# Hybrid attention trunk: query and key tiles in pairs, memory heads first, attention outputs kept in DRAM

## The chip, the cores and the metric

The kernel runs on one core of one Trainium2 chip. The metric is the device time of one execution in microseconds (us); lower is better. Engines are named as in the profile: PE is TensorE (PEld its weight loads), DVE VectorE, ACT ScalarE, POOL GpSimd, SP the SyncE queue from which the loads are issued.

## What is computed

Two layers over 512 tokens of width 2048, all in float32. Cut to what matters here:

```python
for l in range(DEPTH):                                   # 2
    h = rms_norm(x, norm_g[l])
    z = h @ w_in[l]                                      # q, k, v, gate of 6 NA, 6 DL heads; q, gate of 4 memory heads
    o_na = neighbourhood_attention(na_q, na_k, na_v, na_rpb[l])
    o_dl = dilated_attention(rope(dl_q, pos), rope(dl_k, pos), dl_v)
    mk, mv = split(mem_n @ w_mem_kv[l])                  # 256 memory tokens
    o_m = memory_attention(m_q, mk, mv)
    y = concat([o_na * silu(na_g), o_dl * silu(dl_g), o_m * silu(m_g)])
    x = x + y @ w_out[l]
return rms_norm(x, final_g)
```

A head is 128 wide, so it is one column tile of a weight matrix. The contraction over 2048 is cut in 16 k-tiles of 128.

## The kernel before

**Products.** Each float32 operand is split in a high and a low part (`split`, lines 219 to 223: a cast on ACT, a subtraction on DVE). `mm3` (line 243) makes a product with three matmuls: high by high, high by low, low by high. A plain column tile (`gemm_t`) is 16 k-tiles by three matmuls of 512 columns, 48 in all. The values (`gemm_v`) have the tokens as stationary operand and four tiles at once.

**Weights.** They come in halves of 128x1024 in the fixed order `SEQ`; `next_half` loads and splits three halves ahead of the product that uses them. All loads are issued by SP, in program order.

**Pairs.** `gemm_two` makes two column tiles together. Of k-tiles 0 to 7 it takes `PAIRS` = 4 pairs (k, k+4) as two-by-two block matrices: columns of the two tiles, the two halves of the tokens. Seven products of half width (256 columns) stand in the place of eight. Three of the seven use sums of weights (made by `combine` on DVE), three use sums of activations (`mix_pair`), and the parts are added on the way out: `part` is the PSUM bank of the shared products, `e1` and `e2` the corrections, `first` and `second` the main sums. Before, only the gate tiles 4 to 13 and most of the output tiles go in pairs.

**Order.** In a layer: values of heads 0 to 3 (`v0`), NA heads 0 to 3 (q and k each a plain tile), memory values (`mv`), memory keys and queries with their four heads, `v1`, NA 4 and 5, DL 0 and 1, `v2`, DL 2 to 5, 16 gate tiles, 16 output tiles. Attention is not a stage: `attend` (line 405) queues the score products, the transposes and the value products of a head as `steps` that `pump` puts between the matmuls of the next tiles when a running count of PE time (`clock`) reaches them. The times are in `NA_TIMES`, `DIL_TIMES`, `MEM_TIMES`: time to the first score, distance of steps, wait for the transposes. DVE takes the scores out of PSUM with the bias (line 460), ACT does the exponential (line 450), DVE the division (452, 453), PE transposes (418), ACT and DVE split the result (`pth`, `ptl`), PE multiplies by the values into `pv`. A tile scheduler then fixes the order on every engine; each engine works strictly down its own list.

**Norms.** In `v0` the squares are summed in `ssq`; `rms_sums` multiplies them by ones on PE (line 385), a chain of 12 small DVE operations makes the reciprocal root (`rsqrt`, 370 to 376), DVE scales the identity by it (391), and `rms_rows` spreads it over the rows on PE (399). For memory tokens `memory_tile` (line 540) loads two tiles, splits them on ACT and DVE (line 228) and in layer 0 sums squares in `macc` on POOL (365). Before, memory tiles are split beside NA head 3 and `mv`.

**Outputs of attention** stay in SBUF tiles of pool `u` (63 buffers) until the gates multiply them.

Of the kernel before, what the change touches and what calls it, by code (L numbers as in the profile page):

```python
# [33 lines left out]
U_BUFS = 63  # L34
PAIRS = 4
PLAIN = 2
GATES = range(4, 14)
ASIDE = (2, 3)
# [4 lines left out]
NA_TIMES = (5.0, 1.2, 3.0)  # L43
DIL_TIMES = (8.0, 1.3, 4.0)
# [35 lines left out]
def hybrid_kernel(ctx: ExitStack, tc: tile.TileContext, xT, memT, gains, rpbw, wts, cs_tab, dil_tab, na_tab, outT):  # L80
# [65 lines left out]
    for _ in range(WARM):  # L146
        nc.tensor.matmul(bank[:, :P], lhsT=ones, rhs=ones, start=True, stop=True)
    xs = dpool.tile([KO, P, T], F32, tag="xs", name="xs")


    stream = []
    for layer in range(NL):
        at = 0
        two_by_two = {"o": range(PLAIN, KO if layer + 1 < NL else KO - LAST), "g": GATES}
        for key in SEQ:
            tiles = 4 if key[0] in ("v", "mv") else 1
            if key[1] not in two_by_two.get(key[0], ()):
                stream += [(layer, key, (at + i // 2, i % 2)) for i in range(2 * tiles)]
            elif key[1] % 2 == 0:

                two = {}
                stream += [(layer, key, (at, 1)), (layer, key, ("raw", two, at)), (layer, key, (at + 1, 1))]
                stream += [(layer, key, (part, two)) for part in ("sums", "sum", "differences")]
            at += tiles
# [34 lines left out]
    def combine(layer, part, two, at=None):  # L199

        hi, lo = f32rt("wh", W_BUFS, W_HALF), f32rt("wl", W_BUFS, W_HALF)
        if part == "raw":
            a, b, s1 = f32t("wr", W_BUFS, W_HALF), f32t("wr", W_BUFS, W_HALF), tmp()
            two.update(a=a, b=b, s1=s1)
            nc.sync.dma_start(out=a, in_=wts[layer, at, :, :W_HALF])
            nc.sync.dma_start(out=b, in_=wts[layer, at + 1, :, :W_HALF])
            split(a, hi, lo)
            nc.vector.tensor_tensor(s1, b[:, :T], b[:, T:], ALU.add)  # L210
            nc.vector.tensor_tensor(b[:, :T], b[:, :T], a[:, :T], ALU.add)
            nc.vector.tensor_tensor(a[:, :T], a[:, :T], s1, ALU.add)
            nc.vector.tensor_tensor(a[:, T:], a[:, T:], a[:, :T], ALU.add)
            return hi, lo
        if part == "sum":
            return split(two["s1"], hi[:, :T], lo[:, :T])
        return split(two["a" if part == "sums" else "b"], hi, lo)
# [33 lines left out]
    def gemm_t(l, key, act, n=T):  # L251

        acc = acc_bank()
        for half in range(2):
            hi, lo = next_half(l, key)
            for k8 in range(8):
                ko = half * 8 + k8
# [5 lines left out]
    def gemm_two(l, key, act, mixed):  # L263
# [6 lines left out]
        def plain(acc):  # L270
            hi, lo = next_half(l, key)
            for k8 in range(8):
                sl = slice(k8 * P, (k8 + 1) * P)
                mm3(acc, (hi[:, sl], lo[:, sl]), act[8 + k8], k8 == 0, False)
                pump()

        def product(out, w, c0, b, start=False, stop=False, shared=False):
            for i in range(PAIRS):
                sl = slice(c0 + i * P, c0 + (i + 1) * P)
                mm3(out, (w[0][:, sl], w[1][:, sl]), b(i), start and i == 0, stop and i == PAIRS - 1, shared=shared)  # L280
# [8 lines left out]

        e1, e2, u2 = f32t("pth", 2), f32t("pth", 2), tmp(n)  # L290
        plain(first)
        w = next_half(l, key)
        product(part[:, left], w, 0, half_of(0, left), start=True, stop=True, shared=True)
        nc.scalar.copy(e1[:, left], part[:, left])
        product(first[:, left], w, T, half_of(PAIRS, left))
        plain(second)
# [3 lines left out]
        product(first[:, right], w, T, half_of(PAIRS, right), stop=True)  # L300
        product(part[:, right], next_half(l, key), 0, mixed_of(0), stop=True, shared=True)
        nc.vector.tensor_tensor(e1[:, right], part[:, right], u2, ALU.add)
        w = next_half(l, key)
# [3 lines left out]
        product(second[:, left], w, T, mixed_of(2), stop=True)  # L307
        return (first, e1, ALU.add), (second, e2, ALU.subtract)
# [7 lines left out]
    def mix_pair(y, z):  # L316
# [3 lines left out]
        c, d = f32t("p", 4), f32t("p", 4)  # L320
# [84 lines left out]
    def attend(q, score, v, order, first, gap, wait):  # L405
# [16 lines left out]
        def values(n):  # L422
# [22 lines left out]
        return out  # L445
# [18 lines left out]
    def na_head(l, h, q, k, v):  # L464
# [20 lines left out]
        return attend(q, score, v, order, *NA_TIMES)  # L485

    def dil_head(q, k, v):
# [4 lines left out]

        return attend(q, score, v, [(kt, [(qt, kt * P) for qt in range(4)]) for kt in range(4)], *DIL_TIMES)

    def mem_head(q, mk, v):
# [10 lines left out]
        return attend(q, score, v, [(kt, [(qt, kt * P) for qt in range(4)]) for kt in range(2)], *MEM_TIMES)  # L506
# [22 lines left out]
    for l in range(NL):  # L529
# [15 lines left out]
        def beside_first(q):  # L545
# [4 lines left out]
            else:  # L550
# [13 lines left out]
        def beside_mv(q):  # L564
            for _ in range(2 if q in (2, 3) else 0):
                memory_tile()

        def qk_tile(key, scale):
            acc = gemm_t(l, key, act)
            t = tmp()  # L570
            nc.vector.scalar_tensor_tensor(t, acc, scale, rstd, ALU.mult, ALU.mult)
            return split(t, u32r(), u32r())

        def rope_tile(key, scale):
            acc = gemm_t(l, key, act)
            t, u = tmp(), tmp()
            nc.vector.scalar_tensor_tensor(t, acc, scale, rope_c, ALU.mult, ALU.mult)
            nc.vector.scalar_tensor_tensor(u[64:], acc[:64], scale, rope_s[:64], ALU.mult, ALU.mult)
            nc.vector.scalar_tensor_tensor(u[:64], acc[64:], scale, rope_s[64:], ALU.mult, ALU.mult)
            nc.vector.tensor_tensor(t, t, u, ALU.add)  # L580
            return split(t, u32r(), u32r())
# [10 lines left out]
        def memory_heads():  # L592
# [16 lines left out]
            for h in range(H_M):  # L609
                o["m", h] = mem_head(qk_tile(("mq", h), SCALE), mk[h], head_v(mv, h))  # L610

        o = {}
        for n in range(H_NA + H_DL):
            if n == 4:
                memory_heads()
            if n % 4 == 0:
                v = v_split(gemm_v(l, ("v", n // 4), act, 4, beside_first if n == 0 else None,
                                   n == 0 and l == 0), rstd_tok)
                if n == 0:
                    if l == 0:  # L620
                        nc.sync.dma_start(out=namask, in_=na_tab)
                        nc.sync.dma_start(out=dil_sb, in_=dil_tab)
                    nc.sync.dma_start(out=rope_c, in_=cs_tab[0])
                    nc.sync.dma_start(out=rope_s, in_=cs_tab[1])
                    nc.gpsimd.tensor_tensor(rope_c, rope_c, rstd, ALU.mult)
                    nc.gpsimd.tensor_tensor(rope_s, rope_s, rstd, ALU.mult)
            for _ in range(4 if n == 3 else 0):
                memory_tile()
            if n < H_NA:
                q = qk_tile(("naq", n), SCALE)  # L630
                k = qk_tile(("nak", n), 1.0)
                o["na", n] = na_head(l, n, q, k, head_v(v, n % 4))
# [7 lines left out]
        mixed = []  # L640

        def gate(z):

            e = tmp()
            nc.scalar.activation(e, z, AF.Silu)
            y, = o[MIX[len(gated)]]
            out = f32t("ptl", 2) if len(gated) in ASIDE else y
            nc.vector.tensor_tensor(out, y, e, ALU.mult)
            gated.append(out)

        for j in range(KO):
            if j in GATES:
                if j % 2 == 0:
                    for acc, e, op in gemm_two(l, ("g", j), act, mixed):
                        z = f32t("p", 4)
                        nc.vector.tensor_tensor(z, acc, e, op)
                        nc.vector.tensor_tensor(z, z, rstd, ALU.mult)
                        gate(z)
                continue
            acc = gemm_t(l, ("g", j), act)  # L660
            z = tmp()
            nc.vector.tensor_tensor(z, acc, rstd, ALU.mult)
# [204 lines left out]
```

## Time and profile before

| | |
|---|---|
| median of 3 runs | 1847.19 us (1847.12 to 1847.57) |
| the profiled execution's own time | 1847.28 us |
| its span | 1845.5 us |
| PE busy | 1831.0 us, 99% |
| DVE busy | 1086.0 us, 59% |
| ACT busy | 751.1 us, 41% |
| POOL busy | 53.3 us, 3% |
| DMA, mean | 110 GB/s |

The span is the time from the first to the last instruction that the profile holds; the execution's own time is 1.8 us longer. Matmuls overlap at their ends in the trace, so their rate is read from start to start. A busy share is an average over all stages.

### The profile page before, as it was taken

What the parts mean: (1) busy time and instruction counts of PE and PEld (TensorE: products, weight loads), DVE (VectorE), ACT (ScalarE), POOL (GpSimd) and SP (SyncE); (2) the same over time, 40 slices, a digit from 0 to 9 for tenths busy, and PEclk for the clock granted to TensorE, in tenths of its full rate; (3) what the DMA queues carried; (4) which work ended last, traced back from release to release, by engine and by line L of the source; (5) the groups of instructions that cost most, each with busy time, mean ns of one, the idle gap of its engine ahead of it and who ended that gap; (6) DMA issues with size and microseconds to landing.
All of it is one profiled execution on the core that took longest, in us unless ns stands there. A gap on an engine that the chain in (4) does not pass through costs nothing.

```text
span 1845.5 us, 24250 instructions
## 1 busy us (share of the span) xinstructions
PE 1831.0 (99%) x9586; PEld 1569.0 (85%) x9586; DVE 1086.0 (59%) x1803; ACT 751.1 (41%) x1188; POOL 53.3 (3%) x111
## 2 busy tenths in 40 slices
PE   9999999999999999999999999999999999999997
PEld 8888988888888898899888888888888888988987
DVE  7457553463566866666654564435636658676665
ACT  6346442333334434433443453323333444454442
POOL 0113000100000000000000100000000000000000
PEclk9999999999999999999999999999999999999999
DMA  7335423222222233344643353232222222333433
GB/s 283 102 102 156 137 69 98 89 75 86 86 78 81 79 98 121 123 140 160 183 149 96 112 172 114 70 102 81 69 91 80 78 71 80 104 120 115 132 107 110
DMA packets 69201, 202.99 MB, mean 110 GB/s; under 512 B 7264, under 2 KB 16992, under 8 KB 69088
## 3 DMA queue, kind: packets, MB, share of 16 engines
q1 hardware_dynamic: 68800, 201.16, 34.1%
q8 instruction: 75, 1.23, 0.3%
q10 hardware_dynamic: 288, 0.30, 0.1%
q14 instruction: 38, 0.31, 0.1%
HBM read 193.04 MB, written 8.39 MB: 109 GB/s over the span
## 4 chain that ended last, share of the span: by engine, by line
PE 97%; DVE 1%; DMA 0%; issue 0%; ACT 0%; ACTq 0%; DVEq 0%; SPq 0%
PE acc L247 80%; PE sc L247 10%; PE pv L247 4%; PE sc L418 2%; DVE u L228 0%; DVE wl L222 0%; PE acc L342 0%; DVE wr L761 0%; DMA g_sb<-in_gains 0%; DMA u<-in_memT 0%; PE sc L399 0%; PE sc L746 0%; PE sc L385 0%; DVE p L460 0%; ACT u L227 0%
## 5 line engine op out<-in xcount | busy, mean ns | idle before, releaser
L247 PE MATMUL acc<-u,wh 128*128 128x512 f32 (+1 forms) x3976 | 1113.2, 366 | 0.0
L247 PEld LDWEIGHTS acc<-u,wh 128*128 128x128 f32 x3976 | 706.7, 189 | 107.4
L247 PE MATMUL acc<-u,wl 128*128 128x512 f32 (+1 forms) x1988 | 724.7, 365 | 0.0
L222 DVE TENSOR_TENSOR wl<-wr,wh 128x1024 fp32r<-128x1024 f32 (+1 forms) x344 | 420.8, 1223 | 371.9 <-ACT wh L221 370.6
L221 ACT CAST wh<-wr 128x1024 fp32r<-128x1024 f32 (+1 forms) x344 | 360.6, 1048 | 541.4 <-PE acc L247 436.1
L247 PEld LDWEIGHTS acc<-u,wl 128*128 128x128 f32 x1988 | 375.2, 189 | 61.2
L247 PE MATMUL acc<-wh,u 128*128 128x512 f32 x880 | 283.0, 391 | 0.0
L247 PEld LDWEIGHTS acc<-wh,u 128*128 128x128 f32 x880 | 165.2, 188 | 33.7 <-DVE u L228 0.3
L247 PE MATMUL acc<-wl,u 128*128 128x512 f32 x440 | 171.5, 390 | 0.0
L247 PE MATMUL sc<-u,wh 128*128 128x256 f32 x736 | 138.3, 286 | 0.0
L222 DVE TENSOR_TENSOR ptl<-sc,pth 128x512 fp32r<-128x512 f32 (+2 forms) x112 | 67.5, 603 | 93.6 <-ACT pth L221 93.1
L247 PEld LDWEIGHTS sc<-u,wh 128*128 128x128 f32 x736 | 117.3, 191 | 5.2
L221 ACT CAST pth<-sc 128x512 fp32r<-128x512 f32 (+2 forms) x112 | 57.9, 517 | 123.3 <-PE sc L418 122.7
L247 PE MATMUL sc<-u,wl 128*128 128x256 f32 x368 | 104.1, 283 | 0.0
L247 PEld LDWEIGHTS acc<-wl,u 128*128 128x128 f32 x440 | 82.7, 188 | 16.2
L450 ACT ACTIVATE p<-p,stat 128x256 f32<-128x256 f32 (+1 forms) x96 | 59.2, 616 | 86.9 <-DVE stat L460 86.1
L247 PE MATMUL sc<-u,u 128*128 128x256 f32 (+1 forms) x384 | 80.5, 322 | 0.0
L247 PEld LDWEIGHTS sc<-u,u 128*128 128x128 f32 x384 | 65.3, 188 | 11.6
L247 PEld LDWEIGHTS sc<-u,wl 128*128 128x128 f32 x368 | 70.3, 191 | 0.0
L247 PE MATMUL pv<-pth,u 128*128 128x512 f32 (+2 forms) x224 | 68.4, 386 | 0.0
L221 ACT CAST u<-tmp 128x512 fp32r<-128x512 f32 (+1 forms) x64 | 37.9, 592 | 68.9 <-DVE tmp L580 67.2
L418 PEld LDWEIGHTS sc<-ident,p 128*128 128x128 f32 x376 | 47.8, 140 | 15.2 <-DVE p L453 0.6
(137 smaller groups left out, 1201.0 us busy)
## 6 DMA issues: line engine op xcount, KB each, us to landing
wr<-in_wts SPq DMA_DIRECT2D x319, 512.0 KB, 3.6
p<-in_xT SPq DMA_DIRECT2D x23, 256.0 KB, 4.8
p<-xs SPq DMA_DIRECT2D x22, 256.0 KB, 3.4
u<-in_memT SPq DMA_DIRECT2D x16, 256.0 KB, 4.3
xs<-u SPq DMA_DIRECT2D x16, 256.0 KB, 2.0
outT<-wr SPq DMA_DIRECT2D x6, 512.0 KB, 2.9
e<-in_rpbw SPq DMA_DIRECT2D x12, 192.0 KB, 2.4
pth<-in_xT SPq DMA_DIRECT2D x4, 256.0 KB, 4.9
```

The costliest lines, as they stand in the source:

```text
L221: nc.scalar.copy(hi, x)
L222: nc.vector.tensor_tensor(lo, x, hi.bitcast(F32), ALU.subtract)
L247: nc.tensor.matmul(out, lhsT=a[i], rhs=b[j], start=start and n == 0, stop=stop and n == 2, skip_group_check=shared)
L418: nc.tensor.transpose(tr[:, i * P:(i + 1) * P], probs[qt][:, col:col + P], ident)
L450: nc.scalar.activation(s, src, AF.Exp, bias=neg_max, scale=scale, accum_out=l)
```

## The change

1. The two column tiles q and k of each NA and DL head become one pair of `gemm_two` with `QK_PAIRS` = 3 k-pairs: 12 more pairs in a layer. Of the gates tile 0 and 1 (3 k-pairs) and tiles 2 to 13 (4) are pairs; 14 and 15 stay plain.
2. Memory values, keys and queries come right behind `v0`. Memory tiles are split in the second half of `v0` and the first half of `mv`. The sums of activations are built beside the first two memory queries, the fourth behind gate pair 0.
3. `attend` writes a head's output to a DRAM tensor `ys` from ACT's queue (32 writes of 256 KB), and `head` reads it back on SP before the gate (32 reads). The mask of NA and the tables of rope become `u` tiles that are loaded in each layer; the pool has 66.
4. `combine` adds and splits only the columns of the k-pairs taken; the corrections `e1`, `e2` are completed inside `gemm_two`, which hands the result to `take`. The part-left product of its last half is now the last matmul group of a pair.
5. The first score of a head waits longer: `NA_TIMES` 7.0 for 5.0, `DIL_TIMES` 11.0 for 8.0.

```diff
-U_BUFS = 63
+U_BUFS = 66
+QK_PAIRS = 3
 PAIRS = 4
+TWO = {(s, h): QK_PAIRS for s, n in (("naq", 6), ("dlq", 6)) for h in range(n)}
+TWO |= {("g", j): QK_PAIRS if j == 0 else PAIRS for j in range(0, 14, 2)}
-GATES = range(4, 14)
-NA_TIMES = (5.0, 1.2, 3.0)
-DIL_TIMES = (8.0, 1.3, 4.0)
+NA_TIMES = (7.0, 1.2, 3.0)
+DIL_TIMES = (11.0, 1.3, 4.0)
 SEQ = (
     [("v", 0)]
-    + [(s, h) for h in range(4) for s in ("naq", "nak")]
     + [("mv", 0)]
     + [("mk", h) for h in range(H_M)]
     + [("mq", h) for h in range(H_M)]
+    + [(s, h) for h in range(4) for s in ("naq", "nak")]
...
+        if part == "b":
+            split(b[:, c:], hi[:, c:], lo[:, c:])
+            a1, a2, b1, b2 = a[:, :c], a[:, T:T + c], b[:, :c], b[:, T:T + c]
+            for out, x, y in ((b2, b1, b2), (b1, b1, a1), (a1, a1, b2), (a2, a2, a1)):
+                nc.vector.tensor_tensor(out, x, y, ALU.add)
             return hi, lo
...
+        others = [k for k in range(8) if k % 4 >= ns]
+        plain(first, next_half(l, key), range(8), range(8, KO), True)
...
+        product(part[:, right], w, T, mixed_of(0), stop=True, shared=True)
         nc.vector.tensor_tensor(e1[:, right], part[:, right], u2, ALU.add)
         product(part[:, left], w, 0, mixed_of(3), stop=True, shared=True)
         nc.scalar.copy(e2[:, left], part[:, left])
+        nc.vector.tensor_tensor(e1, first, e1, ALU.add)
+        take(0, e1)
         nc.vector.tensor_tensor(e2[:, right], part[:, right], e2[:, left], ALU.add)
+        nc.vector.tensor_tensor(e2, second, e2, ALU.subtract)
+        take(1, e2)
...
                 nc.scalar.copy(out[0], bank[0])
+                nc.scalar.dma_start(out=ys[MIX.index(name)], in_=out[0])
...
+            if q >= 4:
+                memory_tile()
             at = 6 if l == 0 else 3
             if q == at:
                 diag.append(rms_sums(rstd_tok, T, ssq))
...
+        def turned(x, scale):
+            u = tmp()
+            nc.vector.scalar_tensor_tensor(u[64:], x[:64], scale, rope_s[:64], ALU.mult, ALU.mult)
+            nc.vector.scalar_tensor_tensor(u[:64], x[64:], scale, rope_s[64:], ALU.mult, ALU.mult)
+            nc.vector.scalar_tensor_tensor(x, x, scale, rope_c, ALU.mult, ALU.mult)
+            nc.vector.tensor_tensor(x, x, u, ALU.add)
+            return split(x, u32r(), u32r())
+        def qk_tiles(key, rotate):
+            out = []
+            def take(i, x):
+                scale = (SCALE, 1.0)[i]
+                out.append(turned(x, scale) if rotate else scaled(x, scale, x))
+            gemm_two(l, key, act, mixed, QK_PAIRS, take, u32)
+            return out
...
+        def head():
+            y = u32()
+            nc.sync.dma_start(out=y, in_=ys[len(gated)])
+            gated.append(y)
+            return y
```

**How the order moves, first place.** PE in `v0` of layer 0, from the products of the sums of squares (`sc<-ones,ssq`) to the products that spread the result (`sc<-tmp,ones`); `acc` are the four value tiles. Before, 24 matmuls lie between the two (21 of them are left out here):

```order
L385 MATMUL sc_457<-ones,ssq 128x1 x4
L247 MATMUL acc_106<-wh_293,u_396 128x512
...
L247 MATMUL acc_109<-wl_294,u_400 128x512
L247 MATMUL acc_109<-wh_293,u_401 128x512
L399 MATMUL sc_510<-tmp_475,ones 128x128 x4
L247 MATMUL acc_106<-wh_344,u_443 128x512
```

Now:

```order
L256 MATMUL acc_106<-wl_292,u_406 128x512
L407 MATMUL sc_495<-ones,ssq 128x1 x4
L256 MATMUL acc_106<-wh_291,u_407 128x512
...
L256 MATMUL acc_104<-wh_342,u_468 128x512
L256 MATMUL acc_104<-wh_342,u_471 128x512
L421 MATMUL sc_562<-tmp_513,ones 128x128 x4
L256 MATMUL acc_104<-wl_343,u_471 128x512
```

Of the 24 matmuls 14 are left between the two (11 are left out here): the sums moved back by 14 matmuls, into the middle of their half, and the spreading products by four, into the next half.

**Second place.** DVE in the same stretch now; `rs` and `rstd_tok` are the small chain, `u<-u,g_sb,u` is a memory tile's split, `ssq` the squares, the last row scales the identity:

```order
L387 TENSOR_TENSOR ssq<-ssq,tmp_478 128x512
L392 TENSOR_SCALAR rs_500<-sc_495 128x4
L237 SCALAR_TENSOR_TENSOR u_484<-u_481,g_sb,u_483 128x256
L394 TENSOR_SCALAR rstd_tok<-rs_500 128x4
L396 TENSOR_TENSOR rs_502<-rstd_tok 128x4
L237 SCALAR_TENSOR_TENSOR u_484<-u_481,g_sb,u_483 128x256
L397 SCALAR_TENSOR_TENSOR rs_502<-rs_502,rs_500 128x4
L398 SCALAR_TENSOR_TENSOR rstd_tok<-rs_502,rstd_tok 128x4
L396 TENSOR_TENSOR rs_502<-rstd_tok 128x4
...
L413 TENSOR_SCALAR tmp_513<-ident,rstd_tok 128x128 x4
```

Two memory splits stand inside the chain, where before one weight split stood.

**Third place.** DVE in DL head 3 of layer 0; `ptl` is the low part of a transposed block that PE's value product waits for, `wl` a weight half, `u` and `tmp` the rope of the next tile (lines 577 to 580 before). Before:

```order
L580 TENSOR_TENSOR tmp_4838<-tmp_4838,tmp_4839 128x512
L222 TENSOR_TENSOR wl_4851<-wr_4849,wh_4850 128x1024
L222 TENSOR_TENSOR u_4845<-tmp_4838,u_4844 128x512
L222 TENSOR_TENSOR ptl_4879<-sc_4873,pth_4878 128x512
L222 TENSOR_TENSOR wl_4890<-wr_4888,wh_4889 128x1024
L222 TENSOR_TENSOR ptl_4906<-sc_4900,pth_4905 128x512
L222 TENSOR_TENSOR ptl_4926<-sc_4920,pth_4925 128x512
L222 TENSOR_TENSOR ptl_4947<-sc_4941,pth_4946 128x512
L577 SCALAR_TENSOR_TENSOR tmp_4956<-acc_4848,rope_c 128x512
```

Now (lines 601 to 604 are rope, 231 is the split, 222 a sum of weights):

```order
L604 TENSOR_TENSOR u_4789<-u_4789,tmp_4977 128x512
L601 SCALAR_TENSOR_TENSOR tmp_4988<-u_4790,u_3328 64x512
L602 SCALAR_TENSOR_TENSOR tmp_4988<-u_4790,u_3328 64x512
L231 TENSOR_TENSOR u_4983<-u_4789,u_4982 128x512
L603 SCALAR_TENSOR_TENSOR u_4790<-u_4790,u_3327 128x512
L231 TENSOR_TENSOR wl_5001<-wr_4918,wh_5000 128x640
L604 TENSOR_TENSOR u_4790<-u_4790,tmp_4988 128x512
L222 TENSOR_TENSOR wr_4918<-wr_4918 128x384
L231 TENSOR_TENSOR ptl_5037<-sc_5031,pth_5036 128x512
L231 TENSOR_TENSOR u_4994<-u_4790,u_4993 128x512
L222 TENSOR_TENSOR wr_4918<-wr_4918,wr_4916 128x384
L231 TENSOR_TENSOR ptl_5058<-sc_5052,pth_5057 128x512
```

The last two `ptl` of a head stand behind the rope operations of both tiles of the next head, where before the rope of the second tile came behind all four.

## Rows read from the trace of the kernel before

**Rows 1.** The page, parts 1 and 4: busy time of each engine; the chain that ended last by line.

```profile
PE 1831.0 (99%) x9586; PEld 1569.0 (85%) x9586; DVE 1086.0 (59%) x1803; ACT 751.1 (41%) x1188; POOL 53.3 (3%) x111
...
PE acc L247 80%; PE sc L247 10%; PE pv L247 4%; PE sc L418 2%; DVE u L228 0%; DVE wl L222 0%; PE acc L342 0%; DVE wr L761 0%; DMA g_sb<-in_gains 0%; DMA u<-in_memT 0%; PE sc L399 0%; PE sc L746 0%; PE sc L385 0%; DVE p L460 0%; ACT u L227 0
```

**Rows 2.** Timeline of PE in two gate pairs; start us, busy us, engine, line, operation, tiles, count.

```profile
643.10 0.63 PE L247 MATMUL acc<-u,wh 128*128 128x512 f32 x2
...
644.49 0.62 PE L247 MATMUL acc<-u,wh 128*128 128x512 f32 x2
...
648.57 0.40 PE L247 MATMUL sc<-u,wh 128*128 128x256 f32 x2
...
656.90 0.40 PE L247 MATMUL sc<-u,wh 128*128 128x256 f32 x2
...
659.78 0.40 PE L247 MATMUL sc<-u,wh 128*128 128x256 f32 x2
...
664.22 0.63 PE L247 MATMUL acc<-u,wh 128*128 128x512 f32 x2
```

**Rows 3.** Timeline of PE: the first score product of eight heads (256 wide NA, 512 wide DL).

```profile
131.86 0.52 PE L247 MATMUL sc<-u,u 128*128 128x256 f32 x3
...
158.83 0.52 PE L247 MATMUL sc<-u,u 128*128 128x256 f32 x3
...
334.73 0.52 PE L247 MATMUL sc<-u,u 128*128 128x256 f32 x3
...
361.01 0.52 PE L247 MATMUL sc<-u,u 128*128 128x256 f32 x3
...
390.68 0.84 PE L247 MATMUL sc<-u,u 128*128 128x512 f32 x3
...
419.11 0.84 PE L247 MATMUL sc<-u,u 128*128 128x512 f32 x3
...
549.95 0.84 PE L247 MATMUL sc<-u,u 128*128 128x512 f32 x3
...
579.05 0.84 PE L247 MATMUL sc<-u,u 128*128 128x512 f32 x3
```

**Rows 4.** Timeline of PE: value products of the head beside which memory tiles are split.

```profile
171.01 0.38 PE L247 MATMUL pv<-ptl,u 128*128 128x256 f32 x1 [0.29 <-DVE ptl L222]
...
174.44 0.38 PE L247 MATMUL pv<-ptl,u 128*128 128x256 f32 x1 [0.39 <-DVE ptl L222]
```

**Rows 5.** Timeline by engine: the sums of squares and their rows in the first values stage.

```profile
39.34 0.94 PE L385 MATMUL sc<-ones,ssq 128*128 128x1 f32 x8
...
45.73 1.06 PE L399 MATMUL sc<-tmp,ones 128*128 128x128 f32 x8
...
40.32 0.16 DVE L370 TENSOR_SCALAR rs<-sc 128x4 f32<-128x4 f32 x1 [3.81 <-PE sc L385]
...
45.11 0.87 DVE L391 TENSOR_SCALAR tmp<-ident,rstd_tok 128x128 f32<-128x128 f32 x4
```

**Rows 6.** DVE instructions of line 228: nanoseconds min/median/max, first and last start, form.

```profile
L228 DVE SCALAR_TENSOR_TENSOR u<-u,g_sb,u x32: 469/483/1052, 129.2 to 1083.7; 128x256 fp32r<-128x256 f32 x32
```

**Rows 7.** Busy time of each engine in a stretch of four DL heads: PE, PEld, DVE, ACT, POOL.

```profile
482.00:600.00 118.00, 118.00 (x552) 97.27 (x551) 73.81 (x134) 47.77 (x78) 0.00 (x0) 1.00 0.25 80
```

**Rows 8.** Timeline of DVE in a DL head: rope operations one behind the other.

```profile
559.41 0.69 DVE L580 TENSOR_TENSOR tmp<-tmp,tmp 128x512 f32<-128x512 f32 x1
560.01 1.22 DVE L222 TENSOR_TENSOR wl<-wr,wh 128x1024 fp32r<-128x1024 f32 x1
```

**Rows 9.** Groups of DVE and POOL by line and form: busy us, mean ns.

```profile
L222 DVE TENSOR_TENSOR wl<-wr,wh 128x1024 fp32r<-128x1024 f32 x342 | 419.5, 1226 | 366.5 <-ACT wh L221 365.2
L306 DVE TENSOR_TENSOR pth<-sc,pth 128x256 f32<-128x256 f32 x23 | 9.6, 419 | 0.2
L365 POOL TENSOR_TENSOR macc<-macc,tmp 128x256 f32<-128x256 f32 x15 | 14.9, 994 | 35.8 <-ACT tmp L363 35.1
```

**Rows 10.** The page, part 6: DMA issues, KB each, us to landing.

```profile
xs<-u SPq DMA_DIRECT2D x16, 256.0 KB, 2.0
```

More of the change, by code (lines that the diff above doesn't have):

```diff
@@ L153, in hybrid_kernel @@
         at = 0
-        two_by_two = {"o": range(PLAIN, KO if layer + 1 < NL else KO - LAST), "g": GATES}
+        twos = dict(TWO)
+        twos.update({("o", j): PAIRS for j in range(PLAIN, KO if layer + 1 < NL else KO - LAST, 2)})
+        second = False
         for key in SEQ:
             tiles = 4 if key[0] in ("v", "mv") else 1
-            if key[1] not in two_by_two.get(key[0], ()):
+            if second:
+                second = False
+            elif key in twos:
+                two = {"at": at, "ns": twos[key]}
+                stream += [(layer, key, part) for part in (
+                    (at, 1), ("a", two), (at + 1, 1), ("b", two), ("s2 s4", two), ("s1 s3", two))]
+                second = True
+            else:
                 stream += [(layer, key, (at + i // 2, i % 2)) for i in range(2 * tiles)]
[L159 to L163, printed above, removed]
             at += tiles
@@ L256, in gemm_t @@
             for k8 in range(8):
+                if beside is not None and k8 % 4 == 0:
+                    beside()
                 ko = half * 8 + k8
@@ L261, in gemm_t, with gemm_two @@
         return acc
-    def gemm_two(l, key, act, mixed):
+    def gemm_two(l, key, act, mixed, ns, take, tile2=lambda: f32t("pth", 2)):
         first, second, part = acc_bank(), acc_bank(), sc_bank()
@@ L299, in gemm_two, with seldom @@
         nc.scalar.copy(u2, part[:, left])
-        product(first[:, right], w, T, half_of(PAIRS, right), stop=True)
-        product(part[:, right], next_half(l, key), 0, mixed_of(0), stop=True, shared=True)
+        product(first[:, right], w, T, half_of(4, right), stop=True)
+        w = next_half(l, key)
+        product(part[:, right], w, T, mixed_of(0), stop=True, shared=True)
         nc.vector.tensor_tensor(e1[:, right], part[:, right], u2, ALU.add)
-        w = next_half(l, key)
         product(part[:, left], w, 0, mixed_of(3), stop=True, shared=True)
         nc.scalar.copy(e2[:, left], part[:, left])
+        nc.vector.tensor_tensor(e1, first, e1, ALU.add)
+        take(0, e1)
         nc.vector.tensor_tensor(e2[:, right], part[:, right], e2[:, left], ALU.add)
-        product(second[:, left], w, T, mixed_of(2), stop=True)
-        return (first, e1, ALU.add), (second, e2, ALU.subtract)
+        nc.vector.tensor_tensor(e2, second, e2, ALU.subtract)
+        take(1, e2)
+    def seldom(work):
+        turns = iter(range(100))
+        return lambda: work() if next(turns) % 2 else None
     def whole(x):
@@ L402, in rms_rows, with attend @@
         return pb
-    def attend(q, score, v, order, first, gap, wait):
+    def attend(name, q, score, v, order, first, gap, wait):
         out, probs, pts, bank = [], {}, {}, []
@@ L444, in attend @@
         steps.sort(key=lambda s: s[0])
-        return out
     def softmax(s, neg_max, scale, src):
@@ L564, in beside_mv, with scaled, mix_acts @@
         def beside_mv(q):
-            for _ in range(2 if q in (2, 3) else 0):
+            if q < 4:
                 memory_tile()
[L568 to L581, printed above, removed]
+        def scaled(x, scale, out):
+            nc.vector.scalar_tensor_tensor(out, x, scale, rstd, ALU.mult, ALU.mult)
+            return split(out, u32r(), u32r())
+        def turned(x, scale):
[12 more added lines that the diff above has]
+            return out
+        mixed = []
+        def mix_acts():
+            i = len(mixed)
+            if i < QK_PAIRS:
+                mixed.append(mix_pair(whole(act[i]), whole(act[4 + i]), u32))
         def v_split(accs, scales):
@@ L639, in hybrid_kernel @@
         gated = []
-        mixed = []
-        def gate(z):
-            e = tmp()
[L645 to L649, printed above, removed]
-        for j in range(KO):
[L652 to L662, printed above, removed]
-            gate(z)
-            if j + 2 in (GATES[0], GATES[0] + 1):
-                for i in range(PAIRS // 2 * (j + 2 - GATES[0]), PAIRS // 2 * (j + 3 - GATES[0])):
-                    mixed.append(mix_pair(whole(act[i]), whole(act[PAIRS + i])))
+        def head():
[3 more added lines that the diff above has]
+            return y
@@ new lines, in gate @@
+        def gate(z, y):
+            e = tmp()
+            nc.vector.tensor_tensor(e, z, rstd, ALU.mult)
+            nc.scalar.activation(e, e, AF.Silu)
+            nc.vector.tensor_tensor(y, y, e, ALU.mult)
+        for j in range(KO):
+            if ("g", j) in TWO:
+                y = [head(), head()]
+                gemm_two(l, ("g", j), act, mixed, TWO["g", j], lambda i, z: gate(z, y[i]), u32)
+                if j == 0:
+                    for i in range(QK_PAIRS, PAIRS):
+                        mixed.append(mix_pair(whole(act[i]), whole(act[4 + i])))
+            elif ("g", j - 1) not in TWO:
+                y = head()
+                gate(gemm_t(l, ("g", j), act), y)
```

116 lines of the change are left out of this document (55 added, 61 removed).

## The prediction

> **What bounds the kernel now.** I read the busy times first: PE works 99% of the span, DVE 59%, ACT 41%, and the chain that ended last is PE throughout, 80% of it products into `acc` [rows 1]. So the time is PE's matmuls, at the rate at which they can start, plus the few places where PE waits. The reader should then take the rate from the timeline: 18 matmuls of 512 columns lie between 644.49 and 648.57, so 0.2267 us each; 24 of 256 columns between 656.90 and 659.78, so 0.120 each [rows 2]. Two halves thus cost 0.240, not 0.2267. A pair with four k-pairs starts at 643.10 and the next at 664.22: 21.12 [rows 2], where its own matmuls (48 of 512, 84 of 256) make 20.96; 0.16 is lost in it. Two plain tiles are 96 x 0.2267 = 21.76. Last I looked where PE waits: from first score to first score an NA head takes 26.28, one 26.97; a DL head 28.43, some 29.10 [rows 3]. The longer ones hold waits for `ptl`, which DVE makes, as 0.29 and 0.39 at 171 and 174 [rows 4].
>
> The sum is made against the profiled execution's 1847.28 us, 0.09 above the median of the runs, 1847.19.
>
> **Query and key pairs.** With three k-pairs, 36 of 96 wide matmuls go and 63 half-width ones come: 60 x 0.2267 + 63 x 0.120 = 21.16, and 0.16 lost as in the pairs of before: 21.32 for 21.76, 0.44 saved. 24 pairs: **-10.6**. The 0.16 could vanish (-14.4 in all) or double (-6.7).
>
> **Gates.** In each layer one more pair of four (-0.64) and one of three (-0.44): **-2.2**.
>
> The Trainium skill, in "TensorE: Matmul & The Clock Gate", section "Wait — 56ns, not 53.3ns?", gives a warm matmul its columns over 2.4 GHz and about 2.5 ns. By that a product of 512 would be about 215.8 ns and one of 256 about 109.2, and the change (1032 fewer wide, 1806 more narrow) would be worth some 25.5 us, as an estimate, before any loss in the pairs; by the rows the same counts give 17.1. The trace has some 13 ns over the columns for both widths [rows 2], so it disagrees, and the measured rates stay in the sum.
>
> **What the pairs cost DVE.** Per pair: two half-width corrections of 0.42 [rows 9] and two full sums of 0.69; four sums of weights over 384 columns, three quarters of 0.69, so 2.1; and 1152 more split columns at 1.226 per 1024 [rows 9], 1.4. Together 5.7 us, 24 times 137 us: DVE goes from 59% to some 67%. In the DL stretch it worked 73.81 of 118 [rows 7], 18.2 per head; 24 of some 28.4 then, 84%. PE covers this on average, but not where DVE's order puts it ahead of something that PE needs.
>
> **DL heads.** That is the third place of the order: the last two `ptl` of a head stand behind ten to twelve operations for the next head's q and k. I added DVE's rows from the end of the part-right product to each `ptl`, and PE's up to the value product. With each operation at its busy time (0.69) the five heads after the first are late by 1.5, 0.4, 1.2, 0.45 and 1.7, 5.3 us a layer. But operations that follow each other start 0.60 apart (559.41 to 560.01) though they last 0.69 [rows 8]; with eleven of them on that pace each head gains 1.0, and 0.5, 0, 0.2, 0 and 0.7 are left, 1.4 a layer. Before, I count four DL heads at 29.10 for 28.43 [rows 3], 2.7 in all, which go. So between 2.8 - 2.7 = +0.1 and 10.6 - 2.7 = +7.9, and -2.7 if nothing waits. I take 2.5 a layer, nearer the pace that rows show: **+2.3**. The scores themselves are covered: the longer first time in the table leaves 0.5 to 2 us.
>
> **NA heads.** The same walk leaves PE 0.1 to 0.3 late per head, twelve times 1.2 to 3.6; on the measured pace less. **+1**, between -1 and +4. On the other side the memory tiles leave NA head 3, whose period was 0.69 over the others [rows 3] and behind which 0.29 and 0.39 were waited [rows 4]: **-1.4**.
>
> **First values stage.** Here a stall appears. The sums of squares start on PE at 39.34, their chain on DVE at 40.32, and the scaled identity is ready at 45.11 + 0.87 = 45.98 [rows 5]: 6.64 later, of which one weight split is 1.15. Before, PE had the four sums (0.80) and 24 matmuls (5.44) in between, 6.24, and so hardly waited. By the first place of the order it now has 14: 0.80 + 3.17 = 3.97. The chain without the weight split is 5.49, but two memory splits stand in it (second place); one takes 0.48 at the median and up to 1.05 [rows 6], so 6.4 to 7.6. PE waits 2.5 to 3.6, less some 0.2 of before: **+2.6**, once, in layer 0; in layer 1 the order keeps 24 matmuls. The other memory work fills DVE and ACT in a stretch where the weight halves come three ahead; walked row by row, ACT stays about 2 us ahead of PE in `mv`.
>
> The long ones among those splits lie beside POOL's sums of squares, 0.994 each [rows 9]. The Trainium skill, "SBUF — State Buffer", section "🔬 SBUF: two separate sides", says that a DVE operation with two SBUF inputs and a GpSimd operation that reads SBUF take a shared port pair as an exclusive lock for the whole instruction. 0.48 against 1.05 agrees with it; by that rule the small operations of the chain would be held as well, and this stall would be some 3 us longer.
>
> **At nothing.** 32 outputs go to DRAM from ACT's queue and come back through SP; 256 KB took 2.0 us to land [rows 10], the outputs are read many heads later, and the pool slots that the reads wait for are set free long before by the order of the list. If a read did hold the weight loads behind it on SP, one pair would wait some 2 to 4 us per layer. Mask and rope loads are ahead of their use by a head. Building the mixed activations (three times 4.4 us of DVE) has two memory queries, 21.8 us, in which DVE otherwise holds five splits and the scores; it is needed only in the first pair.
>
> **The sum.** -10.6 - 2.2 + 2.3 + 1.0 - 1.4 + 2.6 = -8.3; 1847.28 - 8.3 = **1839.0 us**.
>
> **Rivals.** (1) *DVE becomes the bound of the DL stage, slower.* The rope of q and k now needs a sum in SBUF first, and every link on ACT and DVE is in one line ahead of the last `ptl`; if each of the 12 heads is as late as the worst of the walk, 1.7, that is 20.4 - 2.7 = 17.7 in the place of 2.3: 1854.4. It turns the sign from 1.1 us per head on (10.6 + 2.7 over 12). For it: 84% busy, 1.7 in one head of the walk. Against: at 0.60 from start to start no head comes near. Chance 0.17. (2) *Everything is covered.* No DL or NA head waits, the old waits go too: -10.6 - 2.2 - 2.7 - 1.4 + 2.6 = -14.3, 1833.0; with the loss inside the new pairs gone as well 1828.5. For it: DVE is idle a third of the time. Chance 0.2. (3) *POOL holds DVE.* The chain in `v0` meets four sums of POOL, about 0.8 each, +3.3; NA heads, beside whose bias additions DVE is now fuller, take the +4 of their bound: -8.3 + 3.3 + 3.0 = -2.0, 1845.3. For it: 0.48 against 1.05. Against: those additions were there before, in heads that lost nothing. Chance 0.12. (4) *A read of `ys` holds the weights*, 3.5 a layer: 1846. Against: the slots are free early. Chance 0.04.
>
> **How the numbers follow.** My case has 0.47. A measurement of this kernel tells a change from none at about 0.2%, 3.7 us. Within my case three quarters lie below 1843.5: with the second rival faster is 0.35 + 0.20 = 0.55. The same is 0.11 of my case and most of (3) and (4), 0.24; slower 0.17 and the tails, 0.21. The range: my case with both head terms at their ends is 1832 to 1848; it has to reach rival (2) and most of rival (1): 1829 to 1854.
>
> **What would show it.** Matmul rows: 1032 fewer of 512 and 1806 more of 256 columns, at 0.2267 and 0.120; q and k of a head together 21.3. DVE near 67%. In `v0` of layer 0 a gap of PE of about 3 us before the products that spread the norm. Waits of PE's `pv` products for `ptl` of 3 to 7 us in all, in DL heads. I am wrong if a pair takes over 21.6, if a DL head's period is above 29.5 throughout, or if PE waits for weight halves.

## The result and the profile after

The changed kernel takes **1836.78 us** (1836.56 to 1836.92, 4 runs), the kernel before 1847.15 beside it: 0.9943 of it, 95% interval 0.9926 to 0.9961. That is 10.4 us less, where 8.3 were forecast; the profiled span fell from 1845.5 to 1835.0.

The page after, parts 1 and 4, answers to [rows 1]:

```profile
PE 1816.6 (99%) x10360; PEld 1589.5 (87%) x10360; DVE 1239.2 (68%) x2083; ACT 801.2 (44%) x1324; POOL 50.4 (3%) x111
...
PE 95%; DVE 3%; DMA 1%; ACT 0%; issue 0%; SPq 0%; ACTq 0%; DVEq 0%
```

PE is still the bound: the chain that ended last is PE for 95%, for 97% before. DVE went from 59% to 68%, for the 67% that the prediction counted. The matmuls by form, before and after (count behind the x):

```profile
L247 PE MATMUL acc<-u,wh 128*128 128x512 f32 x3040 | 942.4, 391 | 0.0
L247 PE MATMUL acc<-u,wh 128*128 128x256 f32 x936 | 171.9, 283 | 0.0
L247 PE MATMUL sc<-u,wh 128*128 128x256 f32 x736 | 138.3, 286 | 0.0
```

```profile
L256 PE MATMUL acc<-u,wh 128*128 128x512 f32 x2352 | 731.8, 392 | 0.0
L256 PE MATMUL acc<-u,wh 128*128 128x256 f32 x1452 | 269.7, 283 | 0.0
L256 PE MATMUL sc<-u,wh 128*128 128x256 f32 x1424 | 267.2, 284 | 0.3
```

With the products by `wl`, half as many again, that is 1032 fewer wide and 1806 more narrow, as counted. At the prices of [rows 2], 0.2267 and 0.120, they are worth 17.2 us (the prediction says 17.1), so the change gave back some 6.8. A pair can be timed alone in DL head 2, beside which no attention runs (PE's timeline after, in the columns of [rows 2]):

```profile
458.14 0.62 PE L256 MATMUL acc<-u,wh 128*128 128x512 f32 x2
...
478.23 0.63 PE L256 MATMUL acc<-u,wh 128*128 128x512 f32 x2
...
480.08 0.40 PE L256 MATMUL sc<-u,wh 128*128 128x256 f32 x2
...
481.15 0.40 PE L256 MATMUL acc<-u,wl 128*128 128x512 f32 x1
```

20.09 to the next pair's start, and nine products of its end inside the next pair, 480.08 to 481.15: 21.16, exactly 60 x 0.2267 + 63 x 0.120. In this pair the 0.16 that the prediction gave every pair is not there.

What PE waits for in the whole span, before and then after (us in total, times, longest); one wait of 1.0 at the start, the same in both, is left out:

```profile
PE pv L247 <- DVE ptl L222: 1.1, 3, 0.5
...
PE acc L342 <- ACT u L227: 0.5, 1, 0.5
```

```profile
PE sc L256 <- ACT u L230: 1.5, 2, 0.8
PE pv L256 <- DVE ptl L231: 1.2, 4, 0.4
PE sc L256 <- DVE u L231: 1.2, 2, 0.6
...
PE acc L364 <- ACT u L236: 0.8, 1, 0.8
PE acc L256 <- ACT u L236: 0.2, 1, 0.2
```

New are 2.7 us in which score products (`sc`) wait for a query or key (`u`); no row has a wait for a read of `ys` or for a weight half. They stand at the first score of NA head 4, in both layers. The timeline of PE, DVE and POOL there (in brackets the idle time before, and what ended it):

```profile
333.19 0.38 PE L256 MATMUL sc<-u,u 128*128 128x256 f32 x1 [0.71 <-ACT u L230]
334.15 0.50 PE L256 MATMUL sc<-u,u 128*128 128x256 f32 x2 [0.58 <-DVE u L231]
...
329.04 0.68 DVE L324 TENSOR_TENSOR u<-acc,u 128x512 f32<-128x512 f32 x1
329.64 1.10 DVE L222 TENSOR_TENSOR wr<-wr 128x384 f32<-128x384 f32 x1
330.66 1.78 DVE L595 SCALAR_TENSOR_TENSOR u<-u,rstd 128x512 f32<-128x512 f32 x1
...
329.02 2.87 POOL L671 TENSOR_TENSOR u<-u,rstd 128x512 f32<-128x512 f32 x2 [49.27 <-DMA u<-in_cs]
```

L671 multiplies the two tables of rope by the norm on POOL. While it runs, DVE's weight sum takes 1.10 (0.55 elsewhere) and the scaling of the tile that the score waits for 1.78 (0.69); the line ahead, whose one operand is in PSUM (`acc`), keeps its 0.68.

### The profile page after: what moved, and what is told of

It is laid out like the page before. It is cut to its first block, busy times and chain, and to the rows that moved or that the text cites. A ratio compares the mean times of both kernels' runs of the same rounds, so it can differ in the third digit from the quotient of the medians.

```text
span 1835.0 us, 26369 instructions
## 1 busy us (share of the span) xinstructions
PE 1816.6 (99%) x10360; PEld 1589.5 (87%) x10360; DVE 1239.2 (68%) x2083; ACT 801.2 (44%) x1324; POOL 50.4 (3%) x111
## 4 chain that ended last, share of the span: by engine, by line
PE 95%; DVE 3%; DMA 1%; ACT 0%; issue 0%; SPq 0%; ACTq 0%; DVEq 0%
PE acc L256 72%; PE sc L256 17%; PE pv L256 3%; PE sc L440 2%; DVE wl L231 0%; DVE wr L222 0%; PE acc L364 0%; DVE tmp L602 0%; DVE tmp L601 0%; DVE u L231 0%; ACT wh L230 0%; DVE wr L800 0%; DVE u L603 0%; DMA pth<-xs 0%; DMA g_sb<-in_gains 0%; DVE u L604 0%
## 5 line engine op out<-in xcount | busy, mean ns | idle before, releaser
L256 PE MATMUL acc<-u,wh 128*128 128x512 f32 (+1 forms) x3804 | 999.5, 350 | 0.0
L231 DVE TENSOR_TENSOR wl<-wr,wh 128x1024 fp32r<-128x1024 f32 (+3 forms) x423 | 477.5, 1135 | 406.7 <-ACT wh L230 389.3
L256 PE MATMUL acc<-u,wl 128*128 128x512 f32 (+1 forms) x1902 | 663.6, 349 | 0.0
L230 ACT CAST wh<-wr 128x1024 fp32r<-128x1024 f32 (+3 forms) x423 | 409.6, 975 | 474.3 <-PE acc L256 313.7
L256 PE MATMUL sc<-u,wh 128*128 128x256 f32 x1424 | 267.2, 284 | 0.3
L256 PEld LDWEIGHTS sc<-u,wh 128*128 128x128 f32 x1424 | 224.9, 191 | 14.1 <-DVE u L318 5.1
L256 PE MATMUL sc<-u,wl 128*128 128x256 f32 x712 | 201.2, 283 | 0.0
L256 PEld LDWEIGHTS sc<-u,wl 128*128 128x128 f32 x712 | 135.9, 191 | 0.0
L230 ACT CAST u<-u 128x512 fp32r<-128x512 f32 x92 | 54.5, 619 | 114.1 <-DVE u L604 56.7
L222 DVE TENSOR_TENSOR wr<-wr 128x384 f32<-128x384 f32 (+1 forms) x102 | 64.1, 628 | 0.8
```

What stands on the lines that cost most here:

```text
L222: nc.vector.tensor_tensor(out, x, y, ALU.add)
L230: nc.scalar.copy(hi, x)
L231: nc.vector.tensor_tensor(lo, x, hi.bitcast(F32), ALU.subtract)
L256: nc.tensor.matmul(out, lhsT=a[i], rhs=b[j], start=start and n == 0, stop=stop and n == 2, skip_group_check=shared)
```

## The experiments

Where the time over the price lies is worked out from the trace in one way for all: each matmul's start to the next one's start, less 0.2267, 0.120, 0.1733 (384 columns) or 0.067 (a transpose), summed over a stretch of both layers.

| stretch, both layers | before | queries and keys plain | after | tables on DVE |
|---|---|---|---|---|
| `v0` to `v1` | 15.2 | 13.1 | 13.5 | 14.2 |
| `v1` to `v2` (NA 4, 5, DL 0, 1) | 5.4 | 5.6 | 9.1 | 5.6 |
| `v2` to the layer's end | 13.0 | 12.1 | 17.2 | 17.2 |

The prices leave a rest in attention that nobody waits for: transposes start 0.108 apart, and a DL head of before, 16 transposes and four value products, lies 0.83 over the price without a wait. So work that moves over a boundary moves some of this time with it. From `v2` on there are 80 transposes a layer before and with plain tiles, 88 in the other two columns, because the first scores of DL heads wait longer: half a head more in each layer, some 0.8 us in both as an estimate, which the row above lacks.

**1. Parts of the change.** All queries and keys as plain tiles (`qk_plain`: two `gemm_t`, as before), with the old times to the first score; the rest of the change stays. Then only the DL heads plain, then only the NA heads.

```diff
-TWO = {(s, h): QK_PAIRS for s, n in (("naq", 6), ("dlq", 6)) for h in range(n)}
+TWO = {(s, h): QK_PAIRS for s, n in () for h in range(n)}
...
-                na_head(l, n, *qk_tiles(("naq", n), False), head_v(v, n % 4), namask)
+                na_head(l, n, *qk_plain("na", n, False), head_v(v, n % 4), namask)
...
-NA_TIMES = (7.0, 1.2, 3.0)
-DIL_TIMES = (11.0, 1.3, 4.0)
+NA_TIMES = (5.0, 1.2, 3.0)
+DIL_TIMES = (8.0, 1.3, 4.0)
```

> The changed kernel with all 24 query and key pairs undone (plain tiles and the first times of before; gate pairs, memory first and the DRAM round trip stay). Row price of the pairs alone: 24 x 0.60 = 14.4 us. Theory A (the pairs bring waits of PE with them, some 9 us in DL heads and NA head 4, by their extra DVE work): 14.4 - 9 = +5.5, about 1842. Theory B (the waits come from the new order and go on without the pairs): +14.4, about 1851.

> The changed kernel with only the 12 DL pairs undone. Row price 7.2 us. Theory A: the DL waits of some 5.3 us go with them, so +2, about 1839; waits for ptl in DL heads as before (0.67 in two heads of a layer). Theory B: +7, about 1844.

> The changed kernel with only the 12 NA pairs undone. Row price 7.2 us. Theory A: the wait of NA head 4's first score for its query (1.7 us a layer) goes with them, +3.5, about 1840. Theory B (that wait comes from the values stage ahead, not from the pair): +7, about 1844.

Measured: 1842.02 (1841.57 to 1843.22), 1841.61 (1839.76 to 1842.46) and 1839.97 (1838.45 to 1840.79), beside 1847.58 for the kernel before. So the rest alone is worth 5.6 us, and the 24 pairs 5.2 more, of the 14.4 of their matmuls. By the table the pairs give nothing back in NA heads 0 to 3 (13.1, 13.5), 3.5 us between `v1` and `v2` and 5.1 from `v2` on; with the half head put back it is some 4.3 and 4.3. Theory A's 1842 came, and its 1840 for plain NA heads; for plain DL heads neither 1839 nor 1844 came, but 1841.61. The two halves don't add up (3.2 for the NA pairs, 4.8 for the DL pairs): with plain DL heads the wait at NA 4 grows, to 1.25 and 0.57 in layer 0, and with plain NA heads it is gone.

**2. What makes NA head 4 wait.** Its first score later, then the rope tables one head later, then the tables on DVE.

```diff
-        attend(("na", h), q, score, v, order, *NA_TIMES)
+        attend(("na", h), q, score, v, order, 9.0 if h == 4 else NA_TIMES[0], *NA_TIMES[1:])
```

> The changed kernel with the first score of NA head 4 two units later (9.0 for 7.0), that head alone. If the 0.87 + 0.84 lost there a layer is only a score that comes too early: -3.4 in both layers, about 1833.4. If the query is late for a reason that moves with it, or the shifted steps meet the next head: 0, 1836.8.

```diff
-            if n == H_NA - 1:
+            if n == H_NA:
                 rope_c, rope_s = u32(), u32()
```

> The two tables of rope are loaded and multiplied by the norm on POOL one head later, behind the pair of NA head 5 instead of NA head 4. In the changed kernel POOL multiplies them from 329.02 to 331.89, and in just that time DVE's scaling of head 4's key takes 1.78 us for 0.69 and a weight sum 1.10 for 0.55; PE then waits 0.71 and 0.58 for that query and key. Theory A, POOL's instruction holds DVE's and so makes the wait: without POOL beside them the two DVE instructions take 0.69 and 0.55 again, 1.64 us less, more than the waits; they go in both layers (0.7 + 0.6 and 0.8 + 0.6), 2.7 us: 1836.8 - 2.7 = 1834.1, unless the tables meet as tight a place in the next head. Rival B, the pair ends too late for the first score at 7.0 whatever POOL does: the waits stay, at 1836.8 within 0.5.

```diff
-                    nc.gpsimd.tensor_tensor(table, table, rstd, ALU.mult)
+                    nc.vector.tensor_tensor(table, table, rstd, ALU.mult)
```

> The tables are multiplied on DVE (two instructions, some 0.69 each, 0.60 apart) in the place of POOL; in DVE's order they stand behind the first score's way out of NA head 4. Theory A, the lock: DVE has 1.4 us of work more in each layer and yet the waits of 0.71 and 0.58 go, since 1.64 of holding goes: 1834.1, up to 1835.3 if the other scores of the head wait for the two instructions. Rival B, DVE simply has too much to do there: more work on DVE makes it no better, 1836.8 or up to 1838.

Measured: 1833.88 (1832.72 to 1834.19), 1835.45 (1835.11 to 1836.07) and **1833.98** (1833.35 to 1834.35). A later first score alone thus brings 2.9 of the 3.4 forecast, as much as the tables on DVE. In its timeline POOL still stands beside DVE and the scaling is as slow, but PE has other products until the key is there:

```profile
335.10 0.52 PE L256 MATMUL sc<-u,u 128*128 128x256 f32 x3
...
330.75 1.78 DVE L595 SCALAR_TENSOR_TENSOR u<-u,rstd 128x512 f32<-128x512 f32 x1
```

So the loss takes both, the slow scaling and a first score that leaves no room for it; only the tables on DVE remove the first. In the last one's timeline (PE, then DVE) POOL is idle, the two instructions take 0.55 and 0.68, the score goes without a wait, and the tables cost DVE 1.29:

```profile
332.19 0.68 PE L256 MATMUL sc<-u,u 128*128 128x256 f32 x3
...
329.50 0.55 DVE L222 TENSOR_TENSOR wr<-wr 128x384 f32<-128x384 f32 x1
329.96 0.68 DVE L595 SCALAR_TENSOR_TENSOR u<-u,rstd 128x512 f32<-128x512 f32 x1
...
334.55 1.29 DVE L671 TENSOR_TENSOR u<-u,rstd 128x512 f32<-128x512 f32 x2
```

DVE has four instructions more, 2087 for 2083 by the pages, and the kernel is 2.8 us faster, so not DVE's load but POOL beside it made the wait; in the table `v1` to `v2` falls from 9.1 to 5.6. The run with late tables shows the same hold one head on (PE, DVE, POOL):

```profile
358.40 0.50 PE L256 MATMUL sc<-u,u 128*128 128x256 f32 x2 [0.19 <-DVE u L231]
...
353.31 0.69 DVE L324 TENSOR_TENSOR u<-acc,u 128x512 f32<-128x512 f32 x1
353.91 1.05 DVE L222 TENSOR_TENSOR wr<-wr 128x384 f32<-128x384 f32 x1
354.88 1.80 DVE L595 SCALAR_TENSOR_TENSOR u<-u,rstd 128x512 f32<-128x512 f32 x1
...
352.74 1.81 POOL L672 TENSOR_TENSOR u<-u,rstd 128x512 f32<-128x512 f32 x1 [12.22 <-PE pv L256]
```

There PE waits 0.19 by this row; from start to start it loses 0.35 there and 0.29 at the head's third score, 1.3 in both layers. By that the forecast of 1834.1 was missed: the tables do meet such a place in the next head, as it allowed. That POOL also makes the later loss is not shown.

**3. POOL beside the chain of the norm.** Three bias-sized sums on POOL beside the small chain of `v0` in layer 0.

```diff
                 diag.append(rms_sums(rstd_tok, T, ssq))
+                if l == 0:
...
+                    for i in range(3):
+                        nc.gpsimd.tensor_tensor(beside[:, i * NA_W:(i + 1) * NA_W], ssq[:, :NA_W], ssq[:, NA_W:], ALU.add)
```

> The changed kernel with three additions of 128x256 on POOL in the first values stage of layer 0, started when the sums of squares are complete, as the bias additions of NA head 0 lay there before (their result is not used). Theory lock: three of the twelve small DVE operations take 0.7 us in place of 0.16, as before, the chain lasts 1.5 to 2.5 us longer and PE waits that long ahead of the products that spread the norm: +1.5 to +2.5, about 1839. Theory order (the chain was long before because of the weight split in it): no more than +0.3, 1837.

Measured: 1841.23 (1839.28 to 1841.64), 4.4 over the change; the profiled execution is the fastest of them, with a span 2.5 over that of the change. That one agrees with the +1.5 to +2.5 of the forecast, the median does not; the other four are 1.6 to 2.4 us longer still, and no trace shows by what. The profiled one's timeline (PE, DVE, POOL):

```profile
49.01 1.57 PE L421 MATMUL sc<-tmp,ones 128*128 128x128 f32 x8 [1.90 <-DVE tmp L413]
...
44.39 0.70 DVE L394 TENSOR_SCALAR rstd_tok<-rs 128x4 int32<-128x4 int32 x1
...
46.09 0.69 DVE L397 SCALAR_TENSOR_TENSOR rs<-rs,rs 128x4 f32<-128x4 f32 x1
46.82 0.16 DVE L398 SCALAR_TENSOR_TENSOR rstd_tok<-rs,rstd_tok 128x4 f32<-128x4 f32 x1
...
48.27 1.73 DVE L413 TENSOR_SCALAR tmp<-ident,rstd_tok 128x128 f32<-128x128 f32 x4
...
42.77 2.29 POOL L589 TENSOR_TENSOR nab<-ssq 128x256 f32<-128x256 f32 x3 [3.70 <-ACT tmp L385]
```

An operation on four columns takes 0.7 beside POOL and 0.16 without. The three sums also push back POOL's squares of the memory tiles, which now lie beside the scaling of the identity: 1.73 for 0.87. PE waits 1.90 for it. That is the stall which the prediction had in its sum; here it takes POOL to make it.

**4. DVE's load in DL heads.** The four weight sums of each DL pair left out, then made on POOL (the edit of the second, in part).

```diff
-            for out, x, y in ((b2, b1, b2), (b1, b1, a1), (a1, a1, b2), (a2, a2, a1)):
-                nc.vector.tensor_tensor(out, x, y, ALU.add)
+            add = nc.gpsimd.tensor_tensor if two["dl"] else nc.vector.tensor_tensor
+            for out, x, y in ((b2, b1, b2), (b1, b1, a1), (a1, a1, b2), (a2, a2, a1)):
+                add(out, x, y, ALU.add)
```

> The changed kernel without the four sums of weights of each DL pair (so the DL queries and keys are computed from unsummed weights); the splits and all PE work stay. 2.1 us less DVE work in each of 12 pairs. Theory DVE load: the waits of PE in DL heads (2.6 us a layer more than before) shrink by half or more: -2.5 to -5, about 1833. Theory place (the rope operations and corrections stand ahead of the last ptl whatever the rest is): 0 to -1, 1836.3.

> The changed kernel with the four sums of weights of each DL pair made on POOL in place of DVE. Theory DVE load without contention: -2.5 to -4, about 1833.5. Theory lock (POOL's additions hold DVE's operations for their length, some 1.2 us four times a pair): 0 to +8, 1837 to 1845.

Measured: 1837.1 (1836.63 to 1837.33) without the sums, the time of the change; 1849.37 (1848.64 to 1851.87) with them on POOL, 12.6 more. A waits row of PE and a group of POOL of the second:

```profile
PE sc L257 <- DVE stat L483: 5.6, 6, 1.4
...
L223 POOL TENSOR_TENSOR wr<-wr,wr 128x384 f32<-128x384 f32 x24 | 29.0, 1209 | 1.9
```

Without the sums DVE works 1216.9 us for 1239.2 by its page, and nothing is gained, so these sums' share of its load is not what DL heads lose by. On POOL a sum takes 1.2 for 0.56, and scores wait for DVE's way out; 1849.37 is above the 1845 that the theory of the lock allowed. How much of it is the hold and how much the later weights was not told apart.

**5. Times of the DL heads.** The wait for transposes at 2.5; at 5.5 with late tables; at 5.5 with the tables on DVE.

```diff
-DIL_TIMES = (11.0, 1.3, 4.0)
+DIL_TIMES = (11.0, 1.3, 2.5)
```

> The changed kernel with the transposes of DL heads 1.5 units earlier after the last score (2.5 for 4.0). Theory place: the last blocks then come ahead of the next head's rope operations on DVE, the waits for ptl (0.33 and 0.60 a layer) and some of the small ones go: -1 to -2, about 1835.3. Rival: the transposes now come before the divided scores and PE waits for those: +1 to +4.

> Tables late as in the run before, and the DL heads wait 5.5 in the place of 4.0 before their transposes. Shortening the wait to 2.5 had cost 3 us. Theory A, the value products of DL heads start too early for DVE's low parts (waits of 0.2 to 0.6 in three places of each layer): a longer wait takes these away, 2 to 2.5 us in both layers: 1832. Rival B, the steps then reach into the end of the next pair, where DVE has more ahead of them (rope and corrections): waits come back elsewhere, 1834 or more.

> The tables of rope on DVE, which gave 1833.98, and the DL heads' wait for transposes at 5.5, which beside late tables gave 1834.84 for 1835.45. Theory A, the two act on different stretches and add up: 1834.0 - 0.6 = 1833.4. Rival B, the longer wait was worth nothing (the two intervals, 1835.11 to 1836.07 and 1834.46 to 1835.65, overlap): 1834.0 within 0.4. Rival C, the low parts of DL heads wait for DVE's order and come later with the longer wait: above 1834.4.

Measured: 1839.77 (1839.59 to 1840.05), 1834.84 (1834.46 to 1835.65) and **1833.08** (1832.35 to 1834.15), the fastest kernel of all: 0.9923 of before (0.9909 to 0.9937), 3.7 us under the change. The waits row that comes with 2.5 is

```profile
PE sc L440 <- DVE p L475: 1.7, 6, 0.3
```

(transposes ahead of DVE's division), as the rival said. With late tables 5.5 gave 1834.84, not the 1832 of theory A. The last gain, 0.9 from 4.0 to 5.5 with the tables on DVE, is within the runs' spread: the two intervals overlap, and theory A and rival B are not told apart. The traces of those two say more: with 5.5 PE's waits for `ptl` fall from 1.2 us to 0.3, and yet the stretch from `v2` on is 18.1 over the price for 17.2, the one before it 5.1 for 5.6, and the profiled executions take 1834.15 and 1833.98. Taking the named waits away did not give their time back.

## Why the prediction came near, step by step

The total held, 1836.8 for 1839.0, within the range; several of its terms did not.

**Counts and rates: right.** Counts, 0.2267 and 0.120, DVE's share, and no wait on `ys` or weights.

**"0.16 lost as in the pairs of before": wrong.** The pair that can be timed alone takes 21.16, so at the prices 24 pairs are worth 14.4, not 10.6. The bound "could vanish" was the true end for it. The row was a period of gate pairs, a different pair: 0.10 of its 0.16 is one gap, at 662.56, in the shared products of the pair's end, whose order the change replaces (part 4). A gate pair of four now takes 21.07, from 637.00 to 658.07.

**First values stage, "+2.6": it did not come.** The timeline before, in the stretch of [rows 5], and the same places after:

```profile
40.52 0.17 DVE L372 TENSOR_SCALAR rstd_tok<-rs 128x4 int32<-128x4 int32 x1
40.72 0.70 DVE L374 TENSOR_TENSOR rs<-rstd_tok 128x4 f32<-128x4 f32 x1
...
40.67 2.13 POOL L472 TENSOR_TENSOR nab<-e,namask 128x256 f32<-128x256 f32 x3 [39.19 <-DMA e<-in_rpbw]
```

```profile
42.61 1.05 PE L407 MATMUL sc<-ones,ssq 128*128 128x1 f32 x8
...
46.84 1.16 PE L421 MATMUL sc<-tmp,ones 128*128 128x128 f32 x8
...
44.38 0.16 DVE L396 TENSOR_TENSOR rs<-rstd_tok 128x4 f32<-128x4 f32 x1
...
46.49 0.87 DVE L413 TENSOR_SCALAR tmp<-ident,rstd_tok 128x128 f32<-128x128 f32 x4
```

The 5.49 of "the chain without the weight split" came from a chain that POOL was holding: three of its eleven operations (not twelve) took 0.66 to 0.70, 1.5 us in all over 0.16 each. The memory heads now come first, so POOL's bias sums have moved out of this stretch, and each takes 0.16. The two memory splits cost the chain less than their length: its operations start 0.48 and 0.47 apart around them and 0.20 elsewhere, so 0.6 in all, where the prediction added 0.48 to 1.05 for each. The identity is ready 4.75 after the sums start, not 6.4 to 7.6. And PE need not wait for all four scalings (46.84, before 46.49 + 0.87). From sums to spread it is now 4.23 where 3.97 of matmuls lie between. Rival (3) had the mechanism, but the prediction held POOL's work fixed in time while the change moved it; POOL's queue was not walked.

The Trainium skill, "SBUF — State Buffer", section "Who interferes with whom", says that a DVE instruction with two SBUF inputs contends with a GpSimd instruction that reads SBUF, one with at most one such input and no two-port mode does not. The rows of NA head 4 and of experiment 2 agree: 1.78 for 0.69 with two SBUF inputs, 0.68 and 0.69 with a PSUM operand. L394 of experiment 3 was held with a single SBUF input; the section counts `tensor_scalar` among the operations that can enter a two-port mode, which no run here shows.

**NA heads, "+1": right for four heads, wrong for the fifth.** NA 0 to 3 lose 0.4 in all; between `v1` and `v2` 3.5 are lost in both layers, nearly all at NA 4's first score (0.87 + 0.84 a layer from start to start). Together 3.9, the end of the bound of +4. The walk used DVE's rows alone, and under "At nothing" the prediction costed only the loads of the rope tables. Their product with the norm stood on POOL before as well, but ran as soon as the norm was there:

```profile
L625 POOL TENSOR_TENSOR rope_c<-rope_c,rstd 128x512 f32<-128x512 f32 x2 | 3.5, 1745 | 580.2 <-ACT rstd L401 580.2
```

Part 3 of the change makes the tables `u` tiles of a late head, and so moved it beside the end of NA 4's pair. Experiment 2 shows it by taking it away from POOL; the first score's time of 7.0 left no room for it.

**"Four DL heads at 29.10 for 28.43, 2.7 in all, which go": wrong.** The windows of two such periods before (the stretch, PE's busy time and count):

```profile
483.57:512.00 28.43, 28.43 (x135) 1.00 0.23 74
512.00:541.11 29.11, 29.11 (x138) 1.00 0.23 73
```

The longer one holds three matmuls of 512 more, 3 x 0.2267 = 0.68: it was work on the other side of a boundary, not a wait. Without the 2.7 the term would have been 5.0, and 5.1 were measured against plain tiles from `v2` on. That these agree is luck in part: some 0.8 of the 5.1 is work that moved over a boundary. The mechanism of the third place is seen in DVE's rows and PE's wait after:

```profile
572.95 0.50 PE L256 MATMUL pv<-ptl,u 128*128 128x512 f32 x1 [0.44 <-DVE ptl L231]
...
571.14 0.68 DVE L604 TENSOR_TENSOR u<-u,tmp 128x512 f32<-128x512 f32 x1
571.74 0.55 DVE L222 TENSOR_TENSOR wr<-wr,wr 128x384 f32<-128x384 f32 x1
572.21 0.68 DVE L231 TENSOR_TENSOR ptl<-sc,pth 128x512 fp32r<-128x512 f32 x1
```

The `ptl` stands behind rope and weight sums. But waits named `ptl` make 1.2 us in all, for the 3 to 7 that were to be seen, and experiment 5 took most of them away without a gain that is clear of the spread. The other part of the 5.1 lies in gaps of some 0.1 around value products and first corrections, which no row names. What ends them stays open, and with it whether the place of the `ptl` is what DL heads lose by.

**The rest of the change, in the sum -2.2 - 1.4 + 2.6 = -1.0: measured -5.6.** The gates' matmuls alone, without the 0.16, are -0.80 and -0.60 a layer, -2.8; the stretch `v0` to `v1` lost 2.1 of its time over the price, where the three waits for `ptl` of before, 1.1 by their rows, are gone (the -1.4 was about right); from `v2` on it lost 0.9. The pairs of queries and keys were to give -10.6 + 2.3 + 1.0 = -7.3 and gave -5.2. So -8.3 came near -10.4 partly by luck. The pairs' own loss (3.8), the stall of `v0` (2.6) and the gates (0.6) were priced too dear; the waits of NA heads (2.9) and what DL heads lose (some 2.8) too cheap, and the errors covered each other.

## What to carry to other kernels

Before a duration is carried over, look at what runs beside it on POOL, and ask whether the change moves that: walk POOL's queue as you walk DVE's. Before a longer period is called a wait, count the instructions in both; the same holds for a table by stretches. And a few table products on POOL can cost PE more than the same products on a DVE that is two thirds busy.

## What the runs showed of the hardware

Beside a POOL instruction a DVE instruction on four columns took 0.7 us for 0.16, and one of 512 columns with two SBUF inputs 1.78 for 0.69, but one of 512 with an operand in PSUM its usual 0.68. A matmul of 256 columns costs 0.120 also in a pair of three, without a loss from change of width: 21.16 by price and by trace in the pair that runs alone.
